# One output projection for eight stick-breaking heads, with six heads' outputs waiting in DRAM

## The chip, the cores and the metric

The kernel runs on one core of a Trainium2 chip. The metric is the device time of one execution in microseconds (us). The engines are TensorE (PE; its weight loads are listed as PEld), VectorE (DVE), ScalarE (ACT), GpSimd (POOL) and SyncE (SP), which issues nearly all DMAs.

## The reference, cut to what matters

A decoder trunk of two layers on 1024 tokens and a model width of 1024, in float32. The odd layer's token mixer is stick-breaking attention with 8 heads of 128; its output projection sums over heads and head columns alike, so that it may be summed head by head or in one go:

```python
for i in range(S // BLOCK_Q):                       # blocks of 128 queries
    z = einsum(q[:, lo:hi], k[:, :hi]) * scale
    log_fail = where(strict, -softplus(z), 0.0)
    excl = cumsum(log_fail, reverse=True) - log_fail
    a = where(strict, exp(log_sigmoid(z) + excl), 0.0)
    outs.append(einsum(a, v[:, :hi]))
o = concatenate(outs, axis=1)
h = h + o.reshape(B, S, 1024) @ w_o
```

After the mixer each layer has a cross-attention into 256 memory tokens and a squared-ReLU MLP.

## The kernel before, in words

Activations lie transposed: features on the 128 partitions, tokens along the free dimension, in two halves `c` of 512 tokens. The residual stream is `x[c][f]`, 16 tiles of 128x512 that stay in SBUF. Every float32 operand is split into a rounded high part and a remainder, so that one product is three matmuls (`mm3`, lines 102 to 105, written here as "three matmuls of a step"). A weight block is loaded by `load_w` (line 92): a DMA by SP into a `raw` tile, an ACT copy that makes the high part (line 98), and a POOL subtraction that makes the remainder (line 90, through `split_l`) and with that gives the `raw` tile back.

Tiles are named by tag, and each tag has a fixed number of 128x512 slots (line 37): 32 of `a`, 24 of `g`, 8 of `o`, 6 of `p`, 3 of `raw`, 8 of `w`, 5 of `tmp`; of PSUM banks 3 of `s`, 2 of `pt`, 3 of `acc`. An allocation waits until a slot of its tag is free.

The mixer is `stick` (line 661). Before the loop it projects keys and queries of head 0 and values of heads 0 and 1. Then for each of 8 heads `self_attn` (line 383) is the main work: for each pair of 128-query blocks the scores (line 398), two sigmoids on ACT (lines 458, 459), a scan and a product on DVE (lines 462, 467), transposes on PE (line 420), their eviction, and the products with the values. Beside it runs a "fill", work for PE that does not depend on this head: the keys and queries of the next head (`keys_queries`, 96 steps), in odd heads the values of the next two (`values`, 96), the output projection of the head before (`out_proj`, line 502, 2 times 24), and in the last head the keys and values of the memory tokens (`memory`, line 718, 96) in place of the next head's. `weave` (line 282) takes steps of the fill in proportion to the main work done (an attention counts 77), and `blend` (line 305) mixes two fills in proportion.

`out_proj` for one head: two weight blocks, and for each `c` and each of 8 output blocks `f` three matmuls into a PSUM bank and one DVE addition of that bank to `x[c][f]` (`add_x`, line 255; the addition is line 256):

```python
        def gen(c):
            ...
            for f in range(FT):
                ps = PS("acc")
                mm3(ps, col(w[f // 4][0], f % 4), col(w[f // 4][1], f % 4), o[c][0], o[c][1], True, True)
                add_x(c, f, ps, gcol)
                yield 3
```

Only after the last head's addition is `x[c][f]` final, and `ready` (line 215) then makes the next sub-layer's input: a scaled high part on ACT (line 200), its remainder on DVE (line 201), and the sum of squares (line 132, on POOL or DVE). The second half, `c` = 1, of the last head's projection is handed to `cross` (line 767) as `pending` and blended there with the first two query projections.

Where the attention of a head and its fill leave the order open, it is the framework that lists each engine's instructions, by a simulation of its own (line 1275: `schedule_with_timeline_sim=True`); each engine then runs its list strictly in that order. While the mixer runs, `weight_sums` (line 901) also issues 48 large DMAs, which form sums of weights for the coming MLP; one is taken at every third yield of the main work.

Of the kernel before, what the change touches and what calls it, by code (L numbers as in the profile page):

```python
# [9 lines left out]
F32 = mybir.dt.float32  # L10
F32R = mybir.dt.float32r
# [5 lines left out]
P = 128  # L17
S = 1024
D = 1024
C = 512  # L20
NC_ = S // C
FT = D // P
EPS = 1e-6
QL, KVL = 384, 256
NH = 8
# [28 lines left out]
def trunk_kernel(ctx: ExitStack, tc: tile.TileContext, ins, out):  # L54
    nc = tc.nc
    sb = ctx.enter_context(tc.tile_pool(name="sb", bufs=1))
    pp = ctx.enter_context(tc.tile_pool(name="pp", bufs=1, space=bass.MemoryType.PSUM))
    dr = ctx.enter_context(tc.tile_pool(name="dr", bufs=1, space=bass.MemoryType.DRAM))

    def T(tag, dt=F32):  # L60
        return sb.tile([P, C], dt, tag=tag, name=tag, bufs=SLOTS[tag])

    def PS(tag):
        return pp.tile([P, C], F32, tag="ps_" + tag, name="ps_" + tag, bufs=PSLOTS[tag])
# [27 lines left out]
    def load_w(ap, tag="w"):  # L92

        w = ap.shape[-1]
        raw = T("raw")[:, :w]
        nc.sync.dma_start(out=raw, in_=ap)
        h, l = T(tag, F32R)[:, :w], T(tag, F32R)[:, :w]
        nc.scalar.copy(out=h, in_=raw)  # L98
        split_l(l, raw, h, nc.gpsimd)
        return h, l  # L100
# [6 lines left out]
    def col(w, j, n=P):  # L107
        return w[:, j * n:(j + 1) * n]

    def spread(y, q, r):  # L110

        n = y.shape[-1]
        for t in range(n):
            nc.tensor.transpose(out=col(q, t), in_=y[:, t:t + 1].to_broadcast([P, P]), identity=ident)
        nc.scalar.copy(out=r[:, :n * P], in_=q[:, :n * P])
        return r[:, :n * P]
# [38 lines left out]
    def split(src, tag, eng):  # L155

        w = src.shape[-1]
        h, l = T(tag, F32R)[:, :w], T(tag, F32R)[:, :w]
        nc.scalar.copy(out=h, in_=src)  # L159
        split_l(l, src, h, eng)  # L160
        return h, l

    def steps(ws, per, act, ps):

        kt = len(act)
        for k in range(kt):
            wh, wl = (col(w, k % per) for w in ws[k // per])
            mm3(ps, wh, wl, act[k][0], act[k][1], k == 0, k == kt - 1)
            yield 3
# [85 lines left out]
    def add_x(c, f, ps, gcol=-1):  # L255
        nc.vector.tensor_tensor(out=x[c][f], in0=ps, in1=x[c][f], op=ALU.add)  # L256
        if gcol != -1:
            ready(c, f, gcol)
# [40 lines left out]
    def chain(*parts):  # L299
        def gen():  # L300
            for g, _ in parts:
                yield from g
        return gen(), sum(t for _, t in parts)

    def blend(*parts):

        total = sum(t for _, t in parts)

        def gen():
            live = [[g, 0.0, t] for g, t in parts]  # L310
            while live:
                p = min(live, key=lambda p: p[1] / p[2])
                n = next(p[0], None)
                if n is None:
                    live.remove(p)
                    continue
                p[1] += n
                yield n
        return gen(), total
# [182 lines left out]
    def out_proj(load, o, gcol=-1):  # L502

        w = []

        def gen(c):
            if not w:
                w.extend(load(b) for b in range(2))
# [5 lines that stand above are left out]
        return [(gen(c), 24) for c in range(NC_)]  # L514
# [146 lines left out]
    def stick(gnext):  # L661

        nc.vector.scalar_tensor_tensor(out=mask, in0=ident, scalar=-1e30, in1=mask, op0=ALU.mult, op1=ALU.add)
        a, y, r = zip(*(take(c) for c in range(NC_)))
        scale = float(P ** -0.5)

        def keys_queries(h):
            k, q = [None, None], [None, None]

            def gen():  # L670
                for dst, name in ((k, "w_sk"), (q, "w_sq")):
                    w = [load_w(ins[name][h, j]) for j in range(2)]
                    for c in range(NC_):
                        ps = PS("acc" if h else "s")
                        yield from steps(w, 4, a[c], ps)
                        dst[c] = evict_scaled(ps, r[c], "g", nc.gpsimd)
            return (k, q), (gen(), 96)

        def values(pr):
            def evict(ps, tp):  # L680
                return evict_scaled(ps, per_token(list(zip(y, r)), tp), "g", nc.gpsimd)
            return v_project(lambda b: load_w(ins["w_sv"][pr, b]), 4, 2, a, evict)

        (k, q), part = keys_queries(0)
        run(part)
        v, part = values(0)
        run(part)
        wo = ()
        for h in range(NH):
            hh = h % 2  # L690

            def scores(qb, j, n, k=k, q=q):
                c, s = qb // 4, slice((qb % 4) * P, (qb % 4) * P + P)
                qh, ql = q[c][0][:, s], q[c][1][:, s]
                kh, kl = k[j][0][:, :n], k[j][1][:, :n]
                return [(qh, kh), (qh, kl), (ql, kh)]

            o = [(T("o", F32R), T("o", F32R)) for _ in range(NC_)]
            last = h == NH - 1
            fills, prev = [], wo  # L700
            wo = out_proj(lambda b, h=h: load_w(ins["w_so"][h, b]), o, gnext if last else -1)
            vh = v(hh)
            if last:
                kvm, part = memory(1)
                fills = [blend(chain(*prev), part), wo[0]]
            else:
                if hh:
                    v, part = values((h + 1) // 2)
                    fills.append(part)
                (k, q), part = keys_queries(h + 1)  # L710
                fills.append(blend(chain(*prev), part) if prev else part)
            weave((self_attn(scores, vh, scale, True, o), attn_size(True)), chain(*fills))
        return kvm, wo[1]


    mem_y = []
# [1 line left out]
    def memory(i):  # L718

        km, vm = [], []  # L720

        def gen():
            mn = Norm(D, ML, "a")
            mh = []
            for b in range(4):
                raw = T("raw")
                nc.sync.dma_start(out=raw, in_=ins["memT"][b])
                h2, l2 = T("a", F32R), T("a", F32R)
                for f in range(2):
                    m = col(raw, f, ML)  # L730
                    if i == 0:
                        mn.add(m, nc.gpsimd)
                    gain_split(m, G_MEM + 8 * i + 2 * b + f, col(h2, f, ML), col(l2, f, ML))
                    mh.append((col(h2, f, ML), col(l2, f, ML)))
            for b in range(XH):
                w = [load_w(ins["w_xk"][i, b, j]) for j in range(2)]
                if b % 2 == 0:
                    ps = PS("acc")
                for k in range(FT):
                    mm3(col(ps, b % 2, ML), col(w[k // 4][0], k % 4), col(w[k // 4][1], k % 4), mh[k][0], mh[k][1],  # L740
                        b % 2 == 0 and k == 0, b % 2 == 1 and k == FT - 1)
                yield 12
                if b == 0 and i == 0:
                    my, mr = mn.finish()
                    mem_y.append(my)
                elif b == 0:
                    my = mem_y[0]
                    mr = spread(my, PS("pt"), T("a"))
                if b % 2 == 1:
                    mr2 = mr.rearrange("p (a b) -> p a b", a=1).to_broadcast([P, 2, ML])  # L750
                    km.append(evict_scaled(ps, mr2, "g", nc.gpsimd))
            for b in range(2):
                ps = PS("acc")
                for j in range(4):
                    w = load_w(ins["w_xv"][i, b, j])
                    for t in range(2):
                        ts = slice(t * P, t * P + P)
                        for k in range(2):
                            m = mh[2 * j + k]
                            mm3(col(ps, t, 256), m[0][:, ts], m[1][:, ts], col(w[0], k, 256), col(w[1], k, 256),  # L760
                                j == 0 and t == 0 and k == 0, j == 3 and t == 1 and k == 1)
                    yield 6
                yb = my.rearrange("p (a b) -> p a b", b=1).to_broadcast([P, 2, 256])
                vm.append(evict_scaled(ps, yb, "g", nc.gpsimd))
        return (km, vm), (gen(), 96)
# [431 lines left out]
    kvm = mla(G_CROSS)  # L1197
# [5 lines left out]
    kvm = stick(G_CROSS + 8)  # L1203
# [76 lines left out]
```

## Time and profile before

| | us |
|---|---|
| median of 3 runs | 2677.45 |
| lowest, highest | 2676.29, 2679.50 |
| the profiled execution | 2677.22 |
| its span, first to last instruction | 2675.4 |

The span is 1.8 us shorter than the execution that it was taken from. Busy times in the rows below are per engine; idle time before an instruction is put down to what released it last. In the views of windows each row gives the stretch, its length, and for PE, PEld, DVE, ACT and POOL the busy time with the number of instructions, then the granted clock of PE (1.00 is full speed), the share of the 16 DMA engines in use and the GB/s moved.

### The profile page before, as it was taken

The page shows a single profiled execution, that of the slowest core. Times are in us where ns is not written, and L with a number is a line of the kernel's source. Part 1 is how long each engine was busy: PE and PEld are TensorE (multiplying, and loading weights), DVE is VectorE, ACT ScalarE, POOL GpSimd, SP SyncE. Part 2 cuts the span into 40 slices and gives each one's busy share as a digit, 9 for nine tenths or more (in the row PEclk, how much of TensorE's full clock was granted, in tenths as well). Part 3 has the DMA queues.
Part 4 walks back from the last instruction along what each step waited for, and adds up shares of the span by engine and source line. Part 5 has one row for each costly group of instructions (what it writes and reads, how often), then busy time and mean ns, then how long its engine had stood idle before and what let it go on. Part 6 is the DMA issues. An engine that isn't in the chain of part 4 may idle for free. (4 is left out here: it accounts for less than half of the span.)

```text
span 2675.4 us, 36846 instructions
## 1 busy us (share of the span) xinstructions
PE 2543.8 (95%) x12750; PEld 2119.5 (79%) x12750; DVE 1729.9 (65%) x2866; ACT 1308.4 (49%) x2582; POOL 1365.0 (51%) x1054
## 2 busy tenths in 40 slices
PE   7899999998999999999999999989998999999996
PEld 5788889786788877888888878877876888778885
DVE  6777777857445466556767676687665445576558
ACT  6676676544544554442444333345535454454432
POOL 3543356625744458675523323346248444497653
PEclk9999999999999999999999999999998999999998
DMA  3323456211454466551223234353113545465522
GB/s 121 122 67 106 86 104 154 56 32 43 134 177 153 162 202 190 163 161 57 67 95 118 77 67 92 82 130 79 36 40 100 172 154 169 162 218 168 167 76 75
DMA packets 171178, 310.22 MB, mean 116 GB/s; under 512 B 19184, under 2 KB 61680, under 8 KB 164336
## 3 DMA queue, kind: packets, MB, share of 16 engines
q1 hardware_dynamic: 164704, 278.38, 33.1%
q0 software_dynamic: 6144, 29.36, 6.0%
q8 instruction: 100, 1.64, 0.2%
q14 instruction: 86, 0.70, 0.1%
q10 hardware_dynamic: 144, 0.13, 0.0%
HBM read 248.03 MB, written 118.49 MB: 137 GB/s over the span
## 5 line engine op out<-in xcount | busy, mean ns | idle before, releaser
L90 POOL TENSOR_TENSOR w<-raw,w 128x512 fp32r<-128x512 f32 (+3 forms) x309 | 408.8, 1328 | 470.7 <-ACT w L98 327.0
L90 POOL TENSOR_TENSOR g<-tmp,g 128x512 fp32r<-128x512 f32 x176 | 237.0, 1348 | 289.2 <-ACT g L193 214.5
L103 PE MATMUL ps_acc<-a,w 128*128 128x512 f32 (+1 forms) x801 | 311.4, 389 | 9.9 <-DVE tmp L377 4.7
L104 PE MATMUL ps_acc<-a,w 128*128 128x512 f32 (+1 forms) x801 | 309.7, 387 | 11.2 <-DVE a L90 9.1
L105 PE MATMUL ps_acc<-a,w 128*128 128x512 f32 (+1 forms) x801 | 308.9, 386 | 0.9 <-POOL w L90 0.9
L256 DVE TENSOR_TENSOR x<-ps_acc,x 128x512 f32<-128x512 f32 x312 | 211.8, 684 | 98.9 <-PE ps_acc L105 96.6
L98 ACT CAST w<-raw 128x512 fp32r<-128x512 f32 (+2 forms) x177 | 105.6, 598 | 166.7 <-PE ps_acc L104 108.3
L104 PEld LDWEIGHTS ps_acc<-a,w 128*128 128x128 f32 x801 | 152.1, 190 | 43.3 <-DVE a L90 9.9
L103 PEld LDWEIGHTS ps_acc<-a,w 128*128 128x128 f32 x801 | 152.3, 190 | 42.7 <-DVE tmp L377 5.4
L105 PEld LDWEIGHTS ps_acc<-a,w 128*128 128x128 f32 x801 | 152.2, 190 | 31.2 <-POOL w L90 1.6
L104 PE MATMUL ps_s<-a,w 128*128 128x512 f32 (+1 forms) x386 | 153.7, 398 | 15.3 <-DVE a L90 11.7
L103 PE MATMUL ps_s<-a,w 128*128 128x512 f32 (+1 forms) x386 | 151.9, 397 | 13.3 <-ACT w L98 7.3
L90 DVE TENSOR_TENSOR pt<-ps_pt,pt 128x512 fp32r<-128x512 f32 (+1 forms) x192 | 122.5, 641 | 52.1 <-ACT pt L176 50.8
L176 ACT CAST pt<-ps_pt 128x512 fp32r<-128x512 f32 (+1 forms) x192 | 105.2, 555 | 99.6 <-PE ps_pt L420 59.5
L90 POOL TENSOR_TENSOR a<-p,a 128x512 fp32r<-128x512 f32 x84 | 110.2, 1317 | 82.6 <-ACT a L159 72.4
L105 PE MATMUL ps_s<-a,w 128*128 128x512 f32 (+1 forms) x386 | 151.8, 394 | 0.2 <-POOL w L90 0.2
L90 DVE TENSOR_TENSOR a<-tmp,a 128x512 fp32r<-128x512 f32 x92 | 88.6, 965 | 81.2 <-ACT a L159 80.7
L398 PE MATMUL ps_s<-g 128*128 128x512 f32 (+3 forms) x576 | 137.9, 354 | 3.2 <-ACT p L459 1.7
L159 ACT CAST w<-raw 128x512 fp32r<-128x512 f32 (+3 forms) x132 | 75.7, 574 | 119.4 <-PE ps_acc L104 46.1
L159 ACT CAST a<-tmp 128x512 fp32r<-128x512 f32 x100 | 62.1, 621 | 139.1 <-DMA tmp<-B 127.0
L103 PE MATMUL ps_acc<-o,w 128*128 128x512 f32 x288 | 121.2, 421 | 7.4 <-DVE x L256 7.1
L879 DVE TENSOR_TENSOR p<-p,raw 128x512 f32<-128x512 f32 x56 | 59.3, 1069 | 97.1 <-POOL w L90 70.9
(332 smaller groups left out, 7733.8 us busy)
## 6 DMA issues: line engine op xcount, KB each, us to landing
tmp<-T SPq DMA_DIRECT2D x112, 256.0 KB, 3.0
raw<-in_w_in SPq DMA_DIRECT2D x100, 256.0 KB, 2.8
tmp<-B SPq DMA_DIRECT2D x84, 256.0 KB, 2.9
p<-S_in SPq DMA_DIRECT2D x56, 256.0 KB, 2.9
T<-tmp SPq DMA_DIRECT2D x56, 256.0 KB, 2.6
S_in<-in_w_in SPq DMA_DIRECT2D x12, 1024.0 KB, 6.8
S_out<-in_w_out SPq DMA_DIRECT2D x24, 512.0 KB, 7.4
S_in<-in_w_in POOLq DMA_DIRECT2D x12, 1024.0 KB, 8.2
```

Source lines behind the costliest of these rows:

```text
L90: eng.tensor_tensor(out=l, in0=full, in1=h.bitcast(F32), op=ALU.subtract)
L98: nc.scalar.copy(out=h, in_=raw)
L103: nc.tensor.matmul(out=ps, lhsT=wh, rhs=xh, start=start, stop=False, skip_group_check=True)
L104: nc.tensor.matmul(out=ps, lhsT=wh, rhs=xl, start=False, stop=False, skip_group_check=True)
L105: nc.tensor.matmul(out=ps, lhsT=wl, rhs=xh, start=False, stop=stop, skip_group_check=True)
L159: nc.scalar.copy(out=h, in_=src)
L176: nc.scalar.copy(out=h, in_=ps)
L256: nc.vector.tensor_tensor(out=x[c][f], in0=ps, in1=x[c][f], op=ALU.add)
L398: nc.tensor.matmul(out=ps[:, :n], lhsT=lh, rhs=rh, start=(i == 0), stop=(i == len(passes) - 1), skip_group_check=True)
L879: eng.tensor_tensor(out=out, in0=a, in1=b, op=op)
```

## The change

In `stick` the output projection is no longer a part of each head's fill. The outputs `o` of heads 0 to 5 (four tiles each: two halves `c`, high part and remainder) are written to DRAM right after their head; those of heads 6 and 7 stay in their `o` slots. At the start of the last head `fetch(0, "a")` loads the 12 tiles of `c` = 0 back into `a` slots, and after it `fetch(1, "g")` loads those of `c` = 1 into `g` slots. `out_steps(c)` then sums over all 8 heads in one PSUM bank: 24 matmuls for each `f`, then one `add_x`. It reloads its weights for each `c`: for each `f` two blocks of 4 heads by 128 columns, so that a row of the transfer has four pieces of 512 bytes. One block is split into `w` slots, the other into `p` slots. `out_steps(0)` stands in the last head's fill after `memory`; `out_steps(1)` is what `cross` gets as `pending` (192 steps in place of 24). In `memory` one tile moves from the tag `a` to `tmp`.

```diff
+        heads = []
+
+        def fetch(c, tag):
+            for o in heads[:NH - 2]:
+                ts = [T(tag, F32R) for _ in range(2)]
+                for t, d in zip(ts, o[c]):
+                    nc.sync.dma_start(out=t.bitcast(F32), in_=d)
+                o[c] = ts
+
+        def out_steps(c):
+
+            def gen():
+                for f in range(FT):
+                    w = []
+                    for j in range(2):
+                        raw = T("raw")
+                        nc.sync.dma_start(out=raw.rearrange("p (h c) -> p h c", h=4),
+                                          in_=ins["w_so"][4 * j:4 * j + 4, f // 4, :, (f % 4) * P:(f % 4) * P + P].rearrange("h p c -> p h c"))
+                        w.append(split(raw, "wp"[j], nc.gpsimd))
+                    ps = PS("acc")
+                    yield from steps(w, 4, [o[c] for o in heads], ps)
+                    add_x(c, f, ps, gnext)
+            return gen(), 24 * FT
+
...
-        wo = ()
         for h in range(NH):
...
             o = [(T("o", F32R), T("o", F32R)) for _ in range(NC_)]
+            heads.append(o)
             last = h == NH - 1
-            fills, prev = [], wo
-            wo = out_proj(lambda b, h=h: load_w(ins["w_so"][h, b]), o, gnext if last else -1)
+            fills = []
             vh = v(hh)
             if last:
+                fetch(0, "a")
                 kvm, part = memory(1)
-                fills = [blend(chain(*prev), part), wo[0]]
+                fills = [part, out_steps(0)]
             else:
                 if hh:
                     v, part = values((h + 1) // 2)
                     fills.append(part)
                 (k, q), part = keys_queries(h + 1)
-                fills.append(blend(chain(*prev), part) if prev else part)
+                fills.append(part)
             weave((self_attn(scores, vh, scale, True, o), attn_size(True)), chain(*fills))
-        return kvm, wo[1]
+            if h < NH - 2:
+
+                heads[h] = [[dr.tile([P, C], F32, name=f"o{h}{c}{j}") for j in range(2)] for c in range(NC_)]
+                for c in range(NC_):
+                    for d, t in zip(heads[h][c], o[c]):
+                        nc.sync.dma_start(out=d, in_=t.bitcast(F32))
+        fetch(1, "g")
+        return kvm, out_steps(1)
...
-                    mr = spread(my, PS("pt"), T("a"))
+                    mr = spread(my, PS("pt"), T("tmp"))
```

## Rows read from the trace of the kernel before

**Rows 1.** The page: span, and busy time, share, instructions of each engine.

```profile
span 2675.4 us, 36846 instructions
...
PE 2543.8 (95%) x12750; PEld 2119.5 (79%) x12750; DVE 1729.9 (65%) x2866; ACT 1308.4 (49%) x2582; POOL 1365.0 (51%) x1054
```

**Rows 2.** Windows: the mixer in six stretches, and a stretch of the MLP.

```profile
1338.00:1375.00 37.00, 36.29 (x203) 31.18 (x202) 23.95 (x40) 17.11 (x37) 12.91 (x10) 1.00 0.49 164
1375.00:1504.00 129.00, 128.89 (x773) 113.18 (x772) 93.88 (x158) 52.09 (x115) 39.23 (x29) 1.00 0.27 88
1504.00:1638.00 134.00, 127.05 (x740) 109.86 (x740) 86.44 (x137) 47.13 (x102) 44.43 (x35) 0.99 0.31 71
1638.00:1771.00 133.00, 128.12 (x747) 111.41 (x746) 91.19 (x154) 51.96 (x114) 47.97 (x41) 0.99 0.43 96
1771.00:1828.00 57.00, 52.39 (x368) 47.61 (x367) 44.20 (x67) 27.90 (x58) 33.77 (x27) 1.00 0.54 133
1828.00:1861.00 33.00, 27.78 (x115) 19.59 (x113) 30.83 (x48) 19.27 (x32) 20.75 (x15) 1.00 0.20 49
...
2100.00:2300.00 200.00, 200.00 (x867) 162.56 (x866) 94.15 (x111) 98.70 (x166) 95.79 (x73) 1.00 0.48 156
```

**Rows 3.** Waits of PE, 1306 to 1771: us in total, times, longest.

```profile
PE ps_pt L420 <- DVE p L467: 8.0, 5, 2.2
```

**Rows 4.** Waits of PE, 1771 to 1861.

```profile
PE ps_acc L103 <- DVE x L256: 5.1, 7, 1.3
PE ps_acc L104 <- DVE pt L90: 1.9, 1, 1.9
PE ps_acc L103 <- DVE o L90: 1.3, 1, 1.3
PE ps_acc L104 <- DVE a L201: 1.3, 2, 0.8
```

**Rows 5.** Windows of line 256 alone (DVE busy, count), first pair of heads.

```profile
1375.00:1504.00 129.00, 20.62 (x31) 1.00 0.27 88
```

**Rows 6.** Groups by line and shape, 1306 to 1861: busy us, mean ns; idle before.

```profile
L90 POOL TENSOR_TENSOR w<-raw,w 128x512 fp32r<-128x512 f32 x77 | 109.6, 1435 | 155.0 <-ACT w L98 151.2 <-PE ps_acc L104 3.5
...
L256 DVE TENSOR_TENSOR x<-ps_acc,x 128x512 f32<-128x512 f32 x128 | 86.3, 683 | 49.4 <-PE ps_acc L105 48.5
...
L98 ACT CAST w<-raw 128x512 fp32r<-128x512 f32 x78 | 48.5, 625 | 98.8 <-PE ps_acc L104 74.2 <-issue 9.2 <-PE ps_s L104 3.4
...
L201 DVE SCALAR_TENSOR_TENSOR a<-x,gains,a 128x512 fp32r<-128x512 f32 x15 | 18.3, 1237 | 1.5 <-ACT a L200 1.5
```

**Rows 7.** Timeline in the handover: start, us, instruction, [idle before it <- releaser].

```profile
1832.41 1.81 DVE L201 SCALAR_TENSOR_TENSOR a<-x,gains,a 128x512 fp32r<-128x512 f32 x1
...
1833.21 0.40 PE L105 MATMUL ps_acc<-o,w 128*128 128x512 f32 x1
...
1834.15 1.28 DVE L256 TENSOR_TENSOR x<-ps_acc,x 128x512 f32<-128x512 f32 x2
...
1834.88 0.50 PE L103 MATMUL ps_acc<-o,w 128*128 128x512 f32 x1 [1.27 <-DVE x L256]
```

**Rows 8.** DMA issues: count, KB each, median us from issue to landing.

```profile
tmp<-B SPq DMA_DIRECT2D x84, 256.0 KB, 2.9
...
B<-tmp SPq DMA_DIRECT2D x28, 256.0 KB, 3.0
...
raw<-in_w_so SPq DMA_DIRECT2D x16, 256.0 KB, 2.6
...
raw<-in_w_out SPq DMA_DIRECT2D x56, 64.0 KB, 2.2
```

**Rows 9.** Windows: the stretch with the longest wait of PE in the heads.

```profile
1534.00:1541.00 7.00, 4.11 (x15) 2.80 (x14) 5.75 (x8) 4.17 (x10) 4.57 (x4) 0.76 0.80 246
```

**Rows 10.** Waits of SP's queue, 1690 to 1830.

```profile
SPq L96 <- POOL w L90: 102.5, 27, 22.4
```

## The prediction

> **What bounds the kernel now.** The page comes first: PE is busy 95% of the span and no other engine over 65% [rows 1], so time can come only out of stretches in which PE waits. The windows of the mixer show where these are [rows 2]: length less PE's busy time is 0.7 us in the stretch of head 0, then 0.1, 7.0 and 4.9 us in three stretches of about a pair of heads each, then 4.6 us in the last head and 5.2 us at the handover to the cross-attention. That is 22.5 us in all, and the change cannot win more there, because it leaves the number of matmuls as it is: 8 heads x 2 halves x 8 blocks x 3 = 384 either way. At 200.00/867 = 0.231 us each in a stretch without a gap [rows 2] they are 88.7 us of PE, before and after.
>
> The waits say who is late. In the heads most of it is five waits, 8.0 us, for the DVE product of the stick weights [rows 3]. From the last head on it is 9.6 us, all for DVE: 5.1 for the projection's own additions, the rest for evictions queued beside them [rows 4]. The timeline shows this at work: three matmuls fill a bank in 0.7 us, while DVE spends 1.81 us on one remainder and 1.28 us on two additions, and PE stands 1.27 us for a free bank [rows 7].
>
> **Part by part.**
>
> *Additions.* 128 become 16: 112 x 0.683 us [rows 6] = 76.5 us less on DVE, alone worth nothing to a kernel set by PE. What counts is what PE waited for.
>
> *The heads.* The projections of heads 0 to 5 leave the fills of heads 1 to 6: 6 x 48 x 0.231 = 66.5 us of PE go to the end. In the first pair's stretch DVE is busy 93.88 of 128.89 us of PE, 0.73. Without the additions, 20.62 us there [rows 5], and without two projections, 22.2 us of PE, it is 73.3 of 106.7, 0.69. So DVE is a little less in the way; but the attention's chain also has less to hide under, since heads 2, 4 and 6 keep only 96 fill steps (22.2 us). The nearest row is head 0, which already runs on that fill alone: 0.7 us idle in 37 [rows 2]. Of the 11.9 us idle in the three stretches I take 4 back. Bounds: all 11.9 gained, or, if every stretch comes to lose what the worst one loses, 3 x 7.0 = 21.0, so 9 lost.
>
> *Last head and handover.* An addition with its remainder now comes every 24 matmuls, 5.5 us, and not every 0.7 us; DVE needs 0.683 + 1.237 us for the pair [rows 6]. The waits of rows 4 lose their cause. Of 9.8 us idle I take 8 back; bounds 9.8, and 5.1 if only the waits for line 256 go. What is late next is the chain of the last block, addition, high part, remainder, under the query projections as today.
>
> *Fetch for c = 0.* No row shows it. Twelve tiles of 256 KB are 3.15 MB; at the 246 GB/s seen with the DMA engines 0.80 busy [rows 9] that is 12.8 us, with 2.9 us to landing for a single reload of a spilled tile [rows 8]. The slots come free when the last query projection has done with half 0, one quarter of its 96 steps before the end: 5.5 us of PE, some 10 with the attention woven in. The twelve issues stand on SP ahead of the memory tokens' weights, and the last head's first fill steps wait for those. Behind them the attentions of heads 6 and 7 go on. I take 2 us; bounds 0 (all hidden) and 12.8. The Trainium skill (DMA: Bandwidth & Descriptors, Specifications) puts the fabric's ceiling at 435 GB/s; by it these transfers would be an estimated 7.2 us, the term 0 and the result 2 us lower. No row here shows that rate.
>
> *Fetch for c = 1.* The keys and queries of the last head free 8 `g` slots with the last scores, and the values the rest; by the planner's weights 20 of 77 of the attention is then left and with it 75 of 288 fill steps, 17 us of PE, against the same 12.8 us. I take 0; bound 12.8.
>
> *Weights.* 32 loads in place of 16: 16 more ACT copies at 0.625 us and 16 more POOL subtractions at 1.435 us [rows 6], 10 and 23 us on engines that are 49% and 51% busy. SP waits for POOL to free `raw` tiles as it is [rows 10], but a load takes 2.6 + 0.625 + 1.435 = 4.7 us through one of three tiles, so two pass in 3.1 us, under the 5.5 us of a block. Pieces of 512 bytes: 64 KB blocks, rows of the same 512 bytes, land in 2.2 us [rows 8]; four in series would be 8.8, two loads over three tiles then 7.3 us per block, 1.8 too long. The `p` slots are shared with the attention: worst, each of the last head's 8 blocks waits for one copy and subtraction, 2.1 us. I take 1; bounds 0 and 8 x 2.1 = 17, which also covers the slow pieces.
>
> *Writes of o.* 24 writes, 3.0 us to landing [rows 8]. Each waits for its head's last eviction, and the loads behind it on SP wait with it, then PE for those. Four loads' worth of `w` slots are ahead, so I take 1; bounds 0 and 6 heads x 4.7 = 28. The `o` slots come free sooner than by the projection. The tile moved to `tmp` costs 0: four more `tmp` slots cover it; were they full, one eviction would wait about 1 us.
>
> *Sum:* -4 - 8 + 2 + 0 + 1 + 1 = -8, against the profiled execution 2677.2 - 8 = 2669.2. That execution lies 0.2 us under the median, so I say **2669**. This forecast's own range is -14 to -3.
>
> **The rivals.**
>
> *More goes than that.* All idle of the three stretches and the handover, 11.9 + 9.8 = 21.7 us, goes and every transfer hides: 2655.5. For it: all the large waits name DVE. Against: the heads lose cover too.
>
> *Nothing is left of it.* The 8 us at the handover come back as waits for the fetches and loads: 2672 to 2682. For it: SP's waits for `raw` [rows 10], and the head stretches hardly move. A measurement of this kernel tells about 0.2% (5.4 us) from no change.
>
> *The heads lose their cover (slower).* In heads 2, 4 and 6 only 22.2 us of fill stand beside an attention whose DVE chain is as long as ever. If PE waits there for the product in each of four query pairs as long as in rows 3, that is 3 x 4 x 2.2 = 26 us in place of 8.0, so +18; the other terms give -8 + 2 + 1 + 1 = -4; together 2691. It makes the kernel slower once the idle of the three stretches passes 11.9 + 4 + 5.4 = 21 us. For it: the waits of rows 3 come with a fill half as long again. Against: head 0.
>
> *The fetch is not hidden.* All 12.8 us, in place of 2, in front of the memory tokens' weights, and the clock falls behind the wait: after 2.2 us of waiting the granted clock was 0.76 over 7 us [rows 9], so 48% of them at 1.2 in place of 2.4 GHz, 1.7 us lost. -8 + 10.8 + 1.7 = +4.5: 2682, and slower by more than 0.2% once the weights' path adds 1. The Trainium skill (TensorE: Matmul & The Clock Gate, HAM oscillation) says just this, that a DMA wait between matmuls leaves the next ones cold; row 9 agrees in kind.
>
> **How the numbers follow.** Forecast 0.42, of which 0.05 lies inside 0.2%; more 0.12; nothing left 0.25; cover lost 0.14; fetch not hidden 0.07, counted as slower. Faster: 0.37 + 0.12 = 0.49; within 0.2%: 0.25 + 0.05 = 0.30; slower: 0.21. The range reaches from the middle of the second case to the slower one's figure: 2656 to 2690; half of each of these two, some 0.13, and a little for the weights' and writes' upper bounds lie outside.
>
> **What would show it.** Line 256 with 16 instructions in the mixer; no PE wait for line 256 at the handover; the pair stretches shorter by about 22 us each with idle of about 8 us in all. Wrong would be: waits for line 467 above 20 us (cover lost); PE waiting at the last head's first memory matmuls for line 98 or 90 with SP's twelve fetches ahead; waits of PE for split weights in the `out_steps` blocks.

## The result and the profile after

| | before | after |
|---|---|---|
| median, us | 2678.47 | 2696.95 |
| lowest, highest | 2676.29, 2681.95 | 2694.88, 2701.17 |
| the profiled execution | 2677.22 | 2694.88 |
| its span | 2675.4 | 2693.1 |

The ratio is 1.0068, with a 95% interval of 1.0055 to 1.0081: the change makes the kernel 18.5 us slower, where 8 us faster was forecast. It lies outside the range of 2656 to 2690.

The page of the changed kernel shows the parts that answer to [rows 1]: PE is busy 3.7 us more, DVE 57 us less, POOL 20 us more.

```profile
span 2693.1 us, 36894 instructions
...
PE 2547.5 (95%) x12750; PEld 2123.5 (79%) x12750; DVE 1672.9 (62%) x2754; ACT 1316.5 (49%) x2598; POOL 1385.2 (51%) x1070
```

The windows of the mixer, in the changed kernel, answer to [rows 2]: head 0, two pairs of heads, the third pair with the last head's beginning, the last head, the handover.

```profile
1338.00:1376.00 38.00, 37.29 (x213) 32.22 (x212) 23.91 (x39) 17.73 (x38) 14.21 (x11) 1.00 0.53 177
1376.00:1491.00 115.00, 106.40 (x655) 94.17 (x653) 69.97 (x114) 46.90 (x103) 32.86 (x24) 0.97 0.32 112
1491.00:1607.00 116.00, 106.09 (x647) 93.51 (x647) 68.87 (x112) 45.90 (x100) 37.97 (x30) 0.97 0.35 88
1607.00:1742.00 135.00, 120.89 (x739) 106.63 (x738) 84.80 (x137) 59.28 (x131) 53.75 (x45) 0.96 0.60 142
1742.00:1828.00 86.00, 83.18 (x468) 71.52 (x467) 45.96 (x58) 40.26 (x75) 60.93 (x45) 0.98 0.55 152
1828.00:1900.00 72.00, 70.52 (x330) 57.88 (x329) 36.70 (x72) 29.09 (x58) 31.29 (x24) 1.00 0.22 62
```

The reader is to see that the first two pairs shrink to 115 and 116 us where 22 us of PE work each have left stretches of 129 and 134: 14 and 18 us come off. The rest stayed as idle time. Length less PE's busy time is 0.7 + 8.6 + 9.9 + 14.1 = 33.3 us in the heads, where [rows 2] give 0.7 + 0.1 + 7.0 + 4.9 = 12.7; in the last two stretches it is 2.8 + 1.5 = 4.3 us, where they give 9.8. The granted clock in the heads fell from 0.99 or 1.00 to 0.96 or 0.97 besides.

These stretches do not end at the same place of the program: the third of the pairs reaches 3 us behind the first scores of the last head in the kernel before, and 20 us behind them in the changed one. The same view, cut at each head's first scores, gives for heads 1, 3 and 5 and for the last head with the handover, first before, then after:

```profile
1375.12:1441.78 66.66, 66.57 (x441) 60.52 (x440) 42.79 (x71) 24.75 (x55) 18.91 (x15) 1.00 0.14 44
1490.12:1572.71 82.59, 79.70 (x503) 71.26 (x502) 50.87 (x80) 28.54 (x60) 25.97 (x20) 0.98 0.24 71
1635.31:1703.97 68.66, 67.83 (x442) 61.53 (x441) 43.13 (x73) 25.98 (x55) 25.29 (x22) 1.00 0.34 73
1768.10:1861.00 92.90, 83.07 (x497) 69.78 (x495) 77.44 (x121) 49.60 (x96) 57.02 (x42) 1.00 0.41 101
```

```profile
1376.41:1447.59 71.18, 65.97 (x428) 59.71 (x426) 37.91 (x60) 25.67 (x55) 21.77 (x16) 0.95 0.32 114
1490.70:1563.30 72.60, 66.73 (x428) 59.96 (x427) 36.85 (x60) 25.65 (x54) 23.53 (x18) 0.95 0.27 75
1607.04:1679.49 72.45, 66.58 (x428) 59.88 (x426) 37.57 (x60) 25.64 (x54) 28.92 (x24) 0.95 0.50 106
1722.36:1900.00 177.64, 167.91 (x885) 142.28 (x884) 96.86 (x146) 80.76 (x159) 105.71 (x80) 0.98 0.43 119
```

So heads 1, 3 and 5 stand idle 17.0 us in place of 3.8, heads 2, 4 and 6 (same view) 10.2 in place of 8.1, and the last head with its handover 9.7 in place of 9.8. Nearly all of the loss lies in the odd heads, and the end as a whole won nothing.

PE's waits from 1306 to 1742 answer to [rows 3]:

```profile
PE ps_pt L420 <- DVE p L467: 20.0, 8, 5.1
PE ps_acc L103 <- ACT pt L176: 6.2, 3, 2.8
PE ps_s L398 <- ACT p L459: 3.9, 6, 1.3
PE ps_acc L104 <- DVE pt L90: 2.7, 4, 0.8
```

The wait for the stick weights' product went from 8.0 to 20.0 us, and three of its eight are 5.1 us, at the same place in heads 1, 3 and 5. Another 3.7 us of it, and 1.8 us of the wait for line 459, fall into the first 20 us of the last head. In heads 2, 4 and 6 the changed kernel has no listed wait for line 467; their longest waits, 2.8 us in heads 2 and 4, are for line 176. The waits for line 256 [rows 4] are gone. The timeline of the first 5.1 us wait (last pair of query blocks of head 1):

```profile
1417.36 0.51 PE L398 MATMUL ps_s<-g 128*128 128x384 f32 x2
...
1419.27 3.20 DVE L462 TENSOR_TENSOR_SCAN f<-f,p 128x384 f32<-128x384 f32 x2
...
1420.44 1.55 PE L398 MATMUL ps_s<-g 128*128 128x512 f32 x6
...
1424.95 3.36 DVE L462 TENSOR_TENSOR_SCAN f<-f,p 128x512 f32<-128x512 f32 x2 [1.15 <-ACT p L459]
1425.26 0.38 PE L420 MATMUL ps_pt<-ident,p 128*128 128x128 f32 x2
1425.50 3.87 POOL L90 TENSOR_TENSOR w<-raw,w 128x512 fp32r<-128x512 f32 x2 [4.11 <-PE ps_acc L105]
1428.23 1.68 DVE L467 TENSOR_TENSOR p<-p,f 128x511 f32<-128x511 f32 x1
1429.90 0.68 DVE L467 TENSOR_TENSOR p<-p,f 128x511 f32<-128x511 f32 x1
1430.73 1.51 PE L420 MATMUL ps_pt<-ident,p 128*128 128x128 f32 x6 [5.08 <-DVE p L467]
...
1433.09 0.63 PE L104 MATMUL ps_acc<-a,w 128*128 128x512 f32 x1
1433.51 0.63 PE L105 MATMUL ps_acc<-a,w 128*128 128x512 f32 x1
```

From the first of these scores at 1417.36 to the end of the last product at 1430.58 the chain takes 13 us, two scans of 1.6 to 1.7 us at a time. In between PE had fill steps until 1425.26; then its list has the transposes, and they wait. The next fill steps stand behind them and start after 1432, at a pitch of 0.43 us: after the wait the granted clock is low, here over the 11 us around it.

```profile
1425.00:1436.00 11.00, 5.88 (x21) 4.50 (x20) 7.53 (x8) 2.53 (x5) 5.15 (x3) 0.69 0.62 228
```

The same pair of query blocks in the kernel before:

```profile
1407.82 2.17 PE L398 MATMUL ps_s<-g 128*128 128x512 f32 x9
...
1419.23 0.86 PE L398 MATMUL ps_s<-g 128*128 128x512 f32 x3
...
1429.10 0.82 PE L420 MATMUL ps_pt<-ident,p 128*128 128x128 f32 x6
```

Between its last scores and its six transposes PE has 39 matmuls of fill, 15 of them the projection's (counted in the same timeline), and it waits for nothing. In the changed kernel 15 stand there. A mere exchange of the order could not have filled the whole wait, though: the fill steps behind it read the two weight blocks whose remainders POOL makes in the timeline above, from 1425.50 to 1429.37.

The account of the 17.7 us between the two spans: from the first scores of the mixer (1317.1 before, 1318.4 after) to the last matmul before the first long wait of the MLP that follows the cross-attention (1977.3 and 1992.7) it is 660.2 against 674.3 us, so 14.1 us. 1.3 us arise ahead of the mixer and 2.3 us behind that matmul, where the program's work is the same; why these differ was not tried.

### The profile page after: what moved, and what is told of

Same layout as the page of the kernel before. It is cut to its first block, busy times and chain, and to the rows that moved or that the text cites. A ratio compares the mean times of both kernels' runs of the same rounds, so it can differ in the third digit from the quotient of the medians.

```text
span 2693.1 us, 36894 instructions
## 1 busy us (share of the span) xinstructions
PE 2547.5 (95%) x12750; PEld 2123.5 (79%) x12750; DVE 1672.9 (62%) x2754; ACT 1316.5 (49%) x2598; POOL 1385.2 (51%) x1070
## 5 line engine op out<-in xcount | busy, mean ns | idle before, releaser
L103 PE MATMUL ps_acc<-a,w 128*128 128x512 f32 (+1 forms) x833 | 328.0, 394 | 8.3 <-DVE tmp L377 5.7
L104 PE MATMUL ps_acc<-a,w 128*128 128x512 f32 (+1 forms) x833 | 325.1, 390 | 10.0 <-DVE a L90 9.1
L105 PE MATMUL ps_acc<-a,w 128*128 128x512 f32 (+1 forms) x833 | 324.1, 389 | 1.0 <-POOL w L90 1.0
L104 PEld LDWEIGHTS ps_acc<-a,w 128*128 128x128 f32 x833 | 160.9, 193 | 41.2 <-DVE a L90 9.9
L103 PEld LDWEIGHTS ps_acc<-a,w 128*128 128x128 f32 x833 | 160.8, 193 | 40.3 <-DVE tmp L377 6.3
L105 PEld LDWEIGHTS ps_acc<-a,w 128*128 128x128 f32 x833 | 160.6, 193 | 33.0 <-POOL w L90 1.7
L256 DVE TENSOR_TENSOR x<-ps_acc,x 128x512 f32<-128x512 f32 x200 | 136.3, 685 | 76.6 <-PE ps_acc L105 75.3
L103 PE MATMUL ps_s<-a,w 128*128 128x512 f32 (+1 forms) x386 | 151.1, 395 | 13.2 <-ACT w L98 7.1
L98 ACT CAST w<-raw 128x512 fp32r<-128x512 f32 (+2 forms) x161 | 95.2, 594 | 124.2 <-PE ps_acc L104 49.4
L159 ACT CAST w<-raw 128x512 fp32r<-128x512 f32 (+3 forms) x148 | 85.6, 579 | 138.6 <-PE ps_acc L104 45.8
L90 POOL TENSOR_TENSOR p<-raw,p 128x512 fp32r<-128x512 f32 (+3 forms) x67 | 86.6, 1294 | 101.1 <-ACT p L98 59.3
L462 DVE TENSOR_TENSOR_SCAN f<-f,p 128x128 f32<-128x128 f32 (+3 forms) x96 | 116.7, 1216 | 34.4 <-ACT p L459 33.6
```

The source lines that it names most:

```text
L90: eng.tensor_tensor(out=l, in0=full, in1=h.bitcast(F32), op=ALU.subtract)
L103: nc.tensor.matmul(out=ps, lhsT=wh, rhs=xh, start=start, stop=False, skip_group_check=True)
L104: nc.tensor.matmul(out=ps, lhsT=wh, rhs=xl, start=False, stop=False, skip_group_check=True)
L105: nc.tensor.matmul(out=ps, lhsT=wl, rhs=xh, start=False, stop=stop, skip_group_check=True)
L462: nc.vector.tensor_tensor_scan(out=rev, data0=rev, data1=pt[j][:, :n], op0=ALU.mult, op1=ALU.bypass, initial=1.0 if j == len(pieces) - 1 e ...
```

## The experiments

Two theories stood at the start. **Lost cover:** the projections' matmuls were what PE did while the DVE chain ran, and without them the transposes come up too early in PE's list. **Writes:** the 24 writes stand in SP's queue before the weight loads, which then come late. Ratios are to the kernel before, timed beside each run.

**1. Fewer writes.**

```diff
+                if h:
+                    heads[h] = [list(d) for d in first]
+                    continue
...
+                heads[h] = [list(d) for d in first]
```

> The changed kernel, but only head 0's outputs are written to DRAM (4 writes in place of 24) and heads 1 to 5 are fetched from those same four tiles, so the projection of heads 1 to 5 uses head 0's outputs. Lost cover: the writes are no part of it, 2697 within 4 us, and PE waits for line 467 of about 20 us in the heads as in the changed kernel. Writes in SP's queue hold back the weight loads: 10 to 20 us come back, 2677 to 2687, and the 5.1 us waits of PE shrink.

Measured: 2697.04 us, ratio 1.0071 (1.0054 to 1.0087), and line 467 still makes PE wait 19.2 us.

**2. The writes alone.**

```diff
+            if h < NH - 2:
+                for c in range(NC_):
+                    for j, t in enumerate(o[c]):
+                        nc.sync.dma_start(out=dr.tile([P, C], F32, name=f"o{h}{c}{j}"), in_=t.bitcast(F32))
```

> The kernel before, with the 24 writes of the outputs of heads 0 to 5 added and read by nothing. Lost cover: 2678 within 4 us. Writes in SP's queue: 15 to 20 us slower, 2693 to 2698, with waits in the heads like those of the changed kernel.

Measured: 2676.74 us, ratio 1.0002 (0.9991 to 1.0013). Together with the first: the writes cost nothing that these runs could tell. That theory is out.

**3. Cover given back.**

```diff
+        def idle_steps():
+            for c in range(NC_):
+                for f in range(FT):
+                    ps = PS("acc")
+                    mm3(ps, col(a[c][f][0], 0), col(a[c][f][1], 0), *a[c][f], True, True)
+                    yield 3
...
-                fills.append(part)
+                fills.append(blend((idle_steps(), 48), part) if h else part)
```

> The changed kernel with 288 matmuls more: in heads 1 to 6 the 48 matmuls that were taken out of each fill come back as products of resident activation tiles that nothing reads, without loads, without additions. 288 x 0.231 = 66.5 us of PE are added. Lost cover: most of them run where PE stood waiting, so that the time rises by 66.5 less some 25, to about 2738, and PE waits for line 467 in the heads fall from 20 to under 8 us. Writes or loads hold PE: the waits stay and the time rises by 60 or more, to 2757 to 2765.

Measured: 2719.27 us, ratio 1.0156 (1.0141 to 1.0172). PE's waits in this kernel, 1306 to 1742, all of them:

```profile
PE ps_pt L420 <- DVE p L467: 1.7, 2, 0.9
```

66.5 us of matmuls cost 22.3 us, and the waits for line 467 go, though nothing reads what the matmuls make: this is the run that shows the cover as the cause. The other 44 us, more than the 25 expected, must have found room where PE had stood or crept at a low clock; in the stretch 1376 to 1742, idle fell from 32.6 to 1.0 us:

```profile
1376.00:1742.00 366.00, 364.96 (x2188) 322.51 (x2187) 198.09 (x339) 136.24 (x300) 105.28 (x87) 1.00 0.38 102
```

**4. The additions alone.**

```diff
                 mm3(ps, col(w[f // 4][0], f % 4), col(w[f // 4][1], f % 4), o[c][0], o[c][1], True, True)
-                add_x(c, f, ps, gcol)
+                if gcol != -2:
+                    add_x(c, f, ps, gcol)
...
-            wo = out_proj(lambda b, h=h: load_w(ins["w_so"][h, b]), o, gnext if last else -1)
+            wo = out_proj(lambda b, h=h: load_w(ins["w_so"][h, b]), o, gnext if last else -2)
```

> The kernel before with the 112 additions of heads 0 to 6 of the odd mixer left out, so that their projections never reach the residual stream; the matmuls and loads stay where they are. It prices the DVE part of the change alone, with the cover kept. If the additions matter as the prediction had it: 8 to 15 us faster, 2663 to 2670, the waits for line 256 gone. If they are hidden anyway: 2678 within 4 us.

Measured: 2662.74 us, ratio 0.9944 (0.9929 to 0.9959). So 76.5 us of DVE are worth some 16 us as long as the matmuls stay in the heads, a little more than the 8 to 15 expected. The change gets rid of the same additions, and pays by taking the matmuls along.

**5 and 6. The fill in other places, both kernels.**

```diff
-                yield (5 if not stick else 3) * width / C
+                yield (5 if not stick else 9) * width / C
...
-        return (3 if stick else 5) * 9 + 5 * 10
+        return (9 if stick else 5) * 9 + 5 * 10
```

> The changed kernel, with a block's scores counting 9 in place of 3 in the weave of the stick attention (131 in all in place of 77), so that more of the same fill stands between the scores and the transposes that wait for the DVE chain. No work is added or removed. If the cover is lost because the steps that are left stand in the wrong places: idle of PE in the heads falls from 33 to under 22 us and the time to 2682 to 2690. If there are too few steps, or they cannot run for another reason (no free slot for their results): 2697 within 4 us.

> The control: the same weights of the weave in the kernel before. Its heads stand idle only 11 us, so at most 5 us are to be had: 2672 to 2682 under either theory.

Measured: the changed kernel 2679.06 us, ratio 1.0001 (0.9991 to 1.0011), 18 us better than without the edit and 3 us under the expected range; the kernel before 2686.43 us, ratio 1.0030 (1.0020 to 1.0039), 8 us worse, where 2672 to 2682 was expected; why was not tried. No step was added: place alone gives back what the change lost. The waits for line 467 fall to 3.5 us (1306 to 1850), but those for line 176, the copies that the value products read, rise to 14.2: the steps moved ahead of the transposes are missing behind them.

**7 and 8. Fewer heads joined.** The two kernels keep the head-by-head projection for heads 0 to 5, or 0 to 3.

```diff
+            fills, prev = [], wo
+            wo = ()
+            if h < NH - 2:
+                wo = out_proj(lambda b, h=h: load_w(ins["w_so"][h, b]), o)
...
+                    yield from steps(w, 1, [o[c] for o in heads[6:]], ps)
```

> Heads 0 to 5 are projected head by head, as in the kernel before, and only heads 6 and 7, whose outputs are in their slots anyway, are summed in one bank. Nothing goes to DRAM. Lost cover: the heads keep theirs (waits for line 467 of about 8 us as before), and the additions before the handover are halved, so some 5 to 10 us of the 9.8 us of rows 4 come back: 2668 to 2674. If only the number of additions counts: 16 of 112 are gone, 2 us.

> Heads 0 to 3 head by head, heads 4 to 7 summed at the end (outputs of heads 4 and 5 by way of DRAM). Lost cover: heads 5 and 6 are one pair without cover of three, some 10 of the 30 us that the changed kernel loses in the heads, and the end gains its 18 us as there: 2668 to 2676, between both kernels' parts and below both. If joining itself is bad (transfers, loads at the end), it lies between the two kernels: 2683 to 2692.

Measured: 2688.26 us, ratio 1.0038 (1.0023 to 1.0052), and 2680.45 us, ratio 1.0005 (0.9996 to 1.0015). Both missed. Each has one long wait in the last head. First the kernel with two heads joined, then that with four, waits from 1306 to 1990:

```profile
PE ps_pt L420 <- DVE p L467: 20.1, 7, 8.7
```

```profile
PE ps_pt L420 <- DVE p L467: 9.7, 6, 2.8
PE ps_pt L420 <- ACT a L200: 7.1, 1, 7.1
```

The heads before kept their cover (11.0 us idle from 1376 to 1742 with two joined, 10.0 in the kernel before), but in the last head the transposes again come up before the chain is done, for 8.7 and 7.1 us (the row of the second names line 200, but the product of line 467 ended only 0.14 us before these transposes). It is the same fault in another place; why the list comes out so there was not tried.

**9 to 11. A middle weight, and steps between copy and product.** Besides weight 6, the yield of a value product is split so that half of its steps stand between the eviction and the product (the second edit; the third kernel is the kernel before with both).

```diff
                 evict_split(tp[:, :n], th, tl)
+                if stick:
+                    yield 2.5
...
-                yield 5
+                yield 2.5 if stick else 5
```

> The changed kernel with a block's scores counting 6 in place of 3 in the weave (104 in all). If the place of the fill steps sets the loss, this lies on a curve with 3 (2697) and 9 (2679): 2676 to 2690, with waits for line 467 between 3.5 and 20 us and waits for line 176 between 6 and 14 us. If 9 gained by chance of the listing: anywhere, 2680 to 2700.

> As the one before, and half of the steps that a value product has beside it stand between the transposes' eviction and the product that reads it. Place of the fill: the waits for line 176 (14.2 us at weight 9) fall under 4 us and the time to 2664 to 2674, below both kernels. Too few steps in the heads: what one wait loses another gains, 2676 to 2690.

> The control: the same two edits of the weave in the kernel before. Its heads have the projections as cover in any place: 2670 to 2686. If it gains as much as the changed kernel, the gain there is none of the join.

Measured: 2672.21 us, ratio 0.9975 (0.9964 to 0.9986); 2664.05, ratio 0.9942 (0.9924 to 0.9961); 2663.63, ratio 0.9941 (0.9924 to 0.9959). The first came out 4 us under its expected range. With these edits the changed kernel beats the kernel before, and the kernel before gains as much by the same edits. A twelfth run, the second of these with the joined projection's second weight block in `w` slots for the first half, gave 2664.48, so the shared `p` slots cost nothing that can be told:

> As after_early6_gap, and for the first half the second weight block of the joined projection also goes into w slots, so that it does not share the p slots with the attention. If the p slots hold the last head (4.2 us of waits for their copy at weight 9): 3 to 6 us below after_early6_gap. If not: the same within 3 us.

**13. Chain or slots.** Still open was whether steps were missing, or steps were there that could not run for want of a slot for their result.

```diff
-            nc.vector.tensor_tensor_scan(out=rev, data0=rev, data1=pt[j][:, :n], op0=ALU.mult, op1=ALU.bypass,
...
+            if n != C:
+                nc.vector.tensor_tensor_scan(out=rev, data0=rev, data1=pt[j][:, :n], op0=ALU.mult, op1=ALU.bypass,
...
```

> The changed kernel with the 48 scans of full 512-column pieces left out, so that the stick weights are not the right ones; 63.5 us less on DVE, all of it inside the chain between scores and transposes, nothing else touched. Lost cover (a chain longer than the steps listed beside it): idle of PE in the heads falls from 33 to under 18 us, waits for line 467 from 20 to under 8, time 2672 to 2684. Steps that cannot run for want of slots (g, tmp or PSUM): PE waits as long for something else, 2690 or more.

Measured: 2655.11 us, ratio 0.9916 (0.9899 to 0.9933), 17 us under the expected range. In the waits from 1306 to 1742 no new one takes the place of the old (the product is line 468 here):

```profile
PE ps_pt L420 <- DVE p L468: 4.1, 3, 3.7
PE ps_s L398 <- ACT p L459: 2.2, 4, 0.7
PE ps_acc L103 <- ACT pt L176: 1.0, 3, 0.3
```

Idle from 1376 to 1742 is 366.0 - 357.9 = 8.1 us. With the chain 1.3 us shorter per piece the same steps do run, and 42 us go. So slots for results did not hold them. The 42 us are not the price of the chain's length alone: the run also takes 63.5 us of work from DVE, and run 4 shows that such relief is worth something by itself. That the fill steps behind the long wait get their weights only during it was not tried by itself.

**14 and 15. The split alone,** scores counting 3 as in both kernels.

> The changed kernel with the split of the value product's steps alone (scores still count 3). Place of the fill: the waits for line 176 (7.1 us) go, those for line 467 (20 us) stay, 2686 to 2694.

> The kernel before with the split alone. If its 15 us at weight 6 came from the split: 2662 to 2670. If the weight is needed too: 2672 to 2680.

Measured: 2658.30 us, ratio 0.9925 (0.9910 to 0.9940), and 2657.20, ratio 0.9926 (0.9912 to 0.9941): the shortest times of the runs that leave nothing out, and the expectations missed, by 5 us for the second and by 28 for the first, since there the waits for the product went too (2.5 us are left). But the split also makes more yields, and one in three of these issues a DMA of the weight sums: they were all issued by 1596 us in place of 1813 in the changed kernel, by 1641 in place of 1840 in the kernel before.

**16 and 17. The split at the old pace.**

```diff
-            turn[0] += 1
-            if turn[0] % 3 == 0:
+            turn[0] += n != 2.3
+            if turn[0] % 3 == 0 and n != 2.3:
...
+                    yield 2.3
...
+                yield 2.7 if stick else 5
```

> As after_gap, but the added yields don't count for the weight sums, whose DMAs are issued at the pace of the changed kernel again. If the place of the fill steps alone gained the 39 us: 2658 within 5 us, waits for line 467 under 6 us. If the sooner DMAs gained them: back towards 2697, 2680 or more.

> As before_gap, with the weight sums' DMAs at the old pace. Place of the steps: 2657 within 5 us. Pace of the DMAs: 2670 to 2678.

Measured: the changed kernel 2668.37 us, ratio 0.9966 (0.9953 to 0.9978); the kernel before 2678.20, ratio 1.0002 (0.9992 to 1.0011). So neither expectation for the changed kernel holds whole: of its 39 us, 29 are the place of the steps and 10 the pace. In the kernel before the split gives nothing and the pace all 21. (These two runs yield 2.3 and 2.7 in place of 2.5 twice, a difference taken as nothing.) PE's waits from 1306 to 1742, changed kernel with the split at the old pace, then the kernel before with it:

```profile
PE ps_acc L103 <- ACT pt L176: 4.2, 4, 2.5
PE ps_acc L103 <- DVE o L90: 3.6, 2, 1.8
PE ps_pt L420 <- DVE p L469: 3.2, 3, 2.7
```

```profile
PE ps_acc L103 <- DVE x L256: 5.1, 3, 3.1
PE ps_pt L420 <- DVE p L469: 2.7, 3, 1.3
```

**18. The pace alone,** in the changed kernel, one DMA at every second yield.

```diff
-    aside[0] = weight_sums(1)
+    aside[0], pace[0] = weight_sums(1), 2
```

> The changed kernel with its own weave, no split, and the weight sums' DMAs taken at every second yield of the odd mixer in place of every third, nearly the pace of after_gap. Place of the fill steps as the main cause, pace worth the 10 us that it was with the split: the waits for line 467 stay above 12 us, 2683 to 2692. If the pace does most of it without the split too: 2660 to 2675. If it does nothing without the split: 2697 within 4 us.

Measured: 2685.65 us, ratio 1.0032 (1.0019 to 1.0045), with the waits as they were:

```profile
PE ps_pt L420 <- DVE p L467: 17.3, 7, 5.1
PE ps_acc L103 <- ACT pt L176: 6.1, 3, 2.8
```

Pace and place are thus two gains of their own: some 11 us the one, 29 the other, 39 together. In the changed kernel the sooner DMAs move no wait of these rows by more than 3 us. In the kernel before with the split they do: from the first scores to the MLP, PE's waits for line 256 are 15.5 us at the old pace and 6.3 at the sooner one:

```profile
PE ps_acc L103 <- DVE x L256: 15.5, 12, 3.1
```

```profile
PE ps_acc L103 <- DVE x L256: 6.3, 6, 1.6
```

How the DMAs do this was not tried.

| us | old weave | split, old pace | split, sooner pace |
|---|---|---|---|
| before | 2678.5 | 2678.2 | 2657.2 |
| after | 2697.0 | 2668.4 | 2658.3 |

## Why the prediction was wrong

*What bounds.* Right: PE's waits set the time, and the largest name DVE.

*Additions.* Right that 112 of them go. Taken as worth nothing by themselves, with 4 and 8 us for the waits that they cause; with everything else in place they are worth 16 us (run 4).

*The heads: the step that failed.* I took 4 us back and gave 9 lost as the worst; in the stretches of [rows 2] 20.6 us more were idle, and the clock fell with it. Cut at the heads, 13.2 of these lie in heads 1, 3 and 5, 2.1 in heads 2, 4 and 6, and the rest at the beginning of the last head. The error was to read cover from shares: DVE busy 0.69 of PE's time does not matter where PE runs a fixed list and the chain of one pair of query blocks is 13 us long. What counts is the work listed between the scores and their transposes, and the change cut that: an odd head has 192 matmuls of fill in place of 240, an even one 96 in place of 144, and at the first long wait 15 stand there in place of 39. Head 0, which I took as the nearest row, does not show a head without a projection: its first scores run at 1317 beside the values still being projected, and its last value products beside the next head's.

The rival *cover lost* was right in kind: line 467 makes PE wait 20.0 us in place of 8.0, 12 of the 18 that it priced, the rest came as waits for lines 176 and 459 and as clock, and its threshold of 21 us of idle was passed by 12. It had the place wrong. It priced heads 2, 4 and 6, which have the shortest fill, and these have no listed wait for line 467 at all; the long waits came in heads 1, 3 and 5. So the length of a head's fill does not tell where the wait will be, and why the even heads are spared was not tried. The rival got 0.14, and that its 2691 is only 6 us short is in part luck.

*Last head and handover.* Right for the cause: the waits for line 256 are gone. The gain of 8 did not come: from the last head's first scores on, idle is 9.8 us before and 9.7 after, because 5.5 us of waits for lines 467 and 459 at the beginning of the last head took their place. This head too had lost a projection from its first fill.

*The fetches.* Right that they hide, as far as waits tell; no run was made without them alone. The twelve for `c` = 0 were issued between 1705 and 1712, with 4.6 us to landing in the median, and no wait of PE names them. *Weights:* 3.1 us to landing in place of 2.6, and two waits for `p` tiles, 1.4 and 0.6 us, against 1 forecast. *Writes:* 0 against 1. The DMA groups of the changed kernel:

```profile
raw<-in_w_so SPq DMA_DIRECT2D x32, 256.0 KB, 3.1
...
o<-o SPq DMA_DIRECT2D x24, 256.0 KB, 2.7
...
a<-o SPq DMA_DIRECT2D x12, 256.0 KB, 4.6
g<-o SPq DMA_DIRECT2D x12, 256.0 KB, 4.8
```

*The sum* of -8 came near the worth of the join under another weave, and that by luck, since none of its large terms came as priced: 2668.4 against 2678.2 with the split at the old pace in both. With the sooner pace in both, the two are equal (2658.3 and 2657.2), so even that gain does not hold in every weave.

## What to carry to other kernels

Work that is summed up later is also cover that is taken away earlier: before moving it, measure the longest chain that it hides (here 13 us from scores to transposes) against the work that stays listed inside that chain, at each place where the chain stands, not against busy shares of a stretch or the length of a head's fill. If PE runs a fixed list, try first where the remaining steps stand; one more yield in the right place was worth 29 us here, the change itself minus 18. And test an edit of the order in the kernel before as well: there the same edit gained 21 us for another reason, since it also changed the pace of unrelated DMAs.

## What the runs showed of the hardware

After a wait of 5.1 us PE's matmuls of 512 columns stood 0.43 us apart and not 0.23 for some 2 us, with a granted clock of 0.69 over the 11 us around it: a wait costs more than its own length, since matmuls behind it run at 1.2 in place of 2.4 GHz. In the heads this is likely part of why 44 us of added matmuls were free: with them the clock is 1.00 over 1376 to 1742, without them 0.97.

DVE's scans were slower in the changed kernel though it had less to do: 1471 ns for a 512-column piece (1306 to 1800) where the kernel before has 1323 (1306 to 1861). In the timeline above two of them take 3.36 us while POOL subtracts weights, and a product takes 1.68 us there and 0.68 just after. The two rows of line 462, before and after:

```profile
L462 DVE TENSOR_TENSOR_SCAN f<-f,p 128x512 f32<-128x512 f32 x48 | 63.5, 1323 | 4.5 <-ACT p L459 3.8
```

```profile
L462 DVE TENSOR_TENSOR_SCAN f<-f,p 128x512 f32<-128x512 f32 x48 | 70.6, 1471 | 7.5 <-ACT p L459 6.7
```

In the changed kernel's trace (1306 to 1861) the 26 scans of this size with no subtraction of POOL beside them take 1.21 to 1.29 us each, and every longer one, up to 2.30, has one beside it, though many that have one are not longer. That POOL's work is the cause fits this and was not tried by itself. So a chain's price read from a mean row can be too low just where weight splits fall into it.
